# Interleaving the two chunks of a gating half, and weight buffers assigned by hand

## The chip, the core and the metric

The program runs on one core of a Trainium2 chip. The time is the device time of one execution in microseconds (us). The engines are named as in the profile: PE is the matrix engine (PEld its weight loads), DVE the vector engine, ACT the scalar engine, POOL is GpSimd, SP the engine that issues most transfers.

## What is computed

Two layers of a decoder trunk on 512 tokens of width 1024, all in float32. The change is in the second layer's token mixer, a chunked gating unit:

```python
def chunked_sgu_mixer(h, w_in, ln_g, ln_b, w_spatial, b_spatial, w_out):
    z = jax.nn.gelu(h @ w_in, approximate=False)      # 512 x 1024 @ 1024 x 4096
    u, v = jnp.split(z, 2, axis=-1)
    v = layer_norm(v, ln_g, ln_b)
    mixed = einsum('gts,bcsgd->bctgd', tril(w_spatial), vg) + b_spatial   # 128 x 128 per group
    return (u * mixed) @ w_out                         # 512 x 2048 @ 2048 x 1024
...
# every mixer is followed by:  x + square(relu(h @ w_up)) @ w_down
```

## The kernel before

A float32 product is made of three passes over pairs of fp32r tiles: a high part (`wh`, a cast on ACT, line 125) and a low part (`wl`, a subtraction on DVE, line 122). This is called a split. A large product is done by a seven-product scheme (as Strassen and Winograd), so the work is a list of items. One item multiplies a half-size block, 24 steps of 512 columns or 48 of 256, and needs one weight block of 1 MB (128x2048): loaded by SP, or loaded and then changed by a second transfer that adds another block into it (`add`, issued by POOL), and then split. Sums of products are carried in eight PSUM banks in pairs A, B, C, E. The split tiles `wh` and `wl` have three buffers each, so the split of item j can begin when item j-3 has left PE.

The gating layer (`sgu`, 502.95 us to about 798 us of the span) is 42 items: 0 to 13 the gate half `v` in two chunks of 1024 columns (`gate(0)`, `gate(1)`), 14 to 27 the other half (`other(0)`, `other(1)`), 28 to 41 the output product (`outer`). `prepare` of item j+2 follows `go` of item j in the program. Between items stand steps of the list `then`: `begin` (transposes and splits of the second half of the inputs, `gx1.rest`), the mixing matrix, the deviations, `normalised`, `mixed_tile`, `gated`, and at 40 `gx2.first`, which prepares the next layer's input. Before, the order is

```python
work = g0[:1] + g1[:1] + g0[1:] + g1[1:] + u0 + u1 + dn
```

Raw weight blocks live in a rotating list `raws`: two buffers shared by all layers (`raw_tile`, written R1 and R2 here), one of the layer's own (W), and from item 27 on two halves of `v[1]`. A `get` takes the head of the list, a `put` after the last split appends. `gate(1)` loads its first block, releases it after one item, and loads the same block again for item 9 (`p1` under `if c`).

The last layer (`ffn(1)`) takes its first block (name b) from R1, its second (a) from R2, and the third (c) from its own memory, which lies where the gating layer's tiles were. Item a is a load, an `add` and a split; after it come a sum a += b on DVE, an `add` into b, an `add` into a.

The instructions of each engine stand in one queue and leave it in order. What that order is, the framework's scheduler decides at build time by its own estimates; the program order is its priority. So a load may stand ahead of one that the program names earlier. An instruction waits at the head of its queue until its data and its buffer are ready.

Of the kernel before, what the change touches and what calls it, by code (L numbers as in the profile page):

```python
# [17 lines left out]
P = 128  # L18
# [39 lines left out]
def trunk(ctx: ExitStack, tc: tile.TileContext, a):  # L58
# [914 lines left out]
    class Slots:  # L973
# [5 lines left out]
        def get(self):  # L979
            return self.free.pop(0)  # L980

        def put(self, t):
            self.free.append(t)
# [7 lines left out]
    def ffn(layer, xq, norm, pool, after=None, last=None, mid=None):  # L991
# [7 lines left out]
        w_up, w_dn = a["ffn_w_up"][layer], a["ffn_w_down"][layer]  # L999
        r2, nr2 = small(), small()  # L1000
        raws = Slots(
            [raw_tile((P, 4, 512)) for _ in range(2)]
            + [pool.tile([P, 4, 512], F32, name=nm("wb")) for _ in range(4)]
        )
# [153 lines left out]
        def down(c, sq):  # L1158
# [9 lines left out]
            def fetch(name, k, u):  # L1168
                s[name] = raws.get()
                load(s[name], w(k, u))  # L1170
# [155 lines left out]
    with stage(1), tc.tile_pool(name="sgu", bufs=1) as sg:  # L1326
# [9 lines left out]

        names = ("a11", "a12", "a21", "a22")
        uq = [
            {t: sg.tile([P, 4, H], F32, name=nm("u")) for t in names},
            {t: v[0][:, n, :].rearrange("p (k n) -> p k n", k=4) for n, t in enumerate(names)},  # L1340
        ]
        raws = Slots(
            [raw_tile((P, 4, 512)) for _ in range(2)] + [sg.tile([P, 4, 512], F32, name=nm("wb"))]
        )
        banks = [psum() for _ in range(8)]
# [10 lines left out]

        def staged(i):
            return v[1][:, 2 * i : 2 * i + 2, 512:].rearrange("p a (b t) -> p a b t", t=P)

# [4 lines left out]
        def mix_load():  # L1364
            for gg in range(2):
                nc.gpsimd.dma_start(wsp[:, gg], ws_src[:, gg * 4 : gg * 4 + 4, :])
                nc.gpsimd.dma_start(
                    v[1][:, 2 + gg, 512:], bs_src[gg * 512 : (gg + 1) * 512].partition_broadcast(P)
                )
# [27 lines left out]

        def get(name, src):
            s[name] = raws.get()
            load(s[name], src)  # L1400

        def weights(w, name, make, free, shift=0):

            make()
            w.extend(split(wtiles(4, 512, shift), s[name]))
            if free:
                raws.put(s.pop(name))

        def rows_item(acc, first, left, name, make, free, end, late=None):

            w, l = [], []

            def prepare():
                l.extend(left())
                weights(w, name, make, free)
                if late is not None:
                    late()
# [12 lines left out]

        def cols_item(acc, first, right, name, make, free, end):

# [13 lines left out]

            return lambda: weights(w, name, make, free, 16), go

        norms = {}


        def gate(c, X, Y, Z):
            def w(k, u):
# [28 lines left out]
            def end2():  # L1482
                plus("a11", Z)
                gelu("a11", "r")
# [4 lines left out]
            def end3():  # L1489
                pass  # L1490

            def end6():
                keep("a12", X)
                plus("a12", Y)
                gelu("a12", "nr")
# [7 lines left out]

            def p1():
                if c:
                    get("a", w(0, 0))
                add(s["a"], w(0, 1))

            def p2():
                nc.vector.tensor_add(s["a"], s["a"], s["b"])  # L1510

            def item(acc, first, left, *args):
                return rows_item(acc, first, lambda: getattr(gx1, left), *args)

            return [
                item(X, True, "A11", "d" if c else "a",
                     lambda: get("d" if c else "a", w(0, 0)), bool(c), end1),
                item(Z, True, "A12", "c", lambda: get("c", w(1, 0)), True, end2),
                item(Y, True, "N1", "a", p1, False, end5),
                item(Y, False, "S4", "b", lambda: get("b", w(1, 1)), False, end3, p2),  # L1520
                item(X, False, "S2", "a", lambda: None, False, end6),
                item(X, False, "S3", "b", lambda: add(s["b"], w(0, 1)), True, end7),
                item(X, False, "A22", "a", lambda: add(s["a"], w(1, 0)), True, end4),
            ]


        def other(c, X, Y, Z):
            u = uq[c]

            def w(i, k):  # L1530
# [52 lines left out]
            def p1():  # L1583
                get("a", w(1, 0))
                add(s["a"], w(1, 1))

            def p2():
                nc.vector.tensor_add(s["a"], s["a"], s["b"])

            return [  # L1590
                cols_item(X, True, "A11", "b", lambda: get("b", w(0, 0)), False, end1),
                cols_item(Y, True, "S3", "a", p1, False, end5),
                cols_item(Z, True, "A12", "c", lambda: get("c", w(0, 1)), True, end2),
                cols_item(X, False, "S2", "a", p2, False, end6),
                cols_item(X, False, "N1", "b", lambda: add(s["b"], w(1, 0)), True, end7),
                cols_item(Y, False, "A22", "a", lambda: add(s["a"], w(0, 1)), True, end3),
                cols_item(X, False, "S4", "c", lambda: get("c", w(1, 1)), True, end4),
            ]
# [26 lines left out]
        def outer(X, Y, Z):  # L1625
# [31 lines left out]

            def product(acc, first, left, name, make, free, end, extra=None, late=None):
                for h in range(2):
                    def lefts(h=h):  # L1660
                        if extra is not None:
                            extra(h)
                        pairs.append(pairs.pop(0))
                        return split(pairs[-1], q[h][left])

                    items.append(rows_item(
                        acc, first and h == 0, lefts, f"{name}{h}", lambda h=h: make(h), free,
                        end if h else lambda: None,
                        (lambda h=h: late(h)) if late is not None else None,
                    ))  # L1670

            def put(n, k, u):
                return lambda h: get(f"{n}{h}", w(k, h, u))

# [3 lines left out]
            def p2(h):  # L1678
                nc.vector.tensor_add(s[f"a{h}"], s[f"a{h}"], s[f"b{h}"])

            product(X, True, "a11", "a", put("a", 0, 0), False, lambda: accumulate(X, 0, 0, 1))
            product(
                Z, True, "a12", "c", put("c", 1, 0), True, lambda: accumulate(Z, 0, 0, 1, True)
            )
            product(
                Y, True, "n1", "a", sum_("a", 0, 1), False, lambda: accumulate(Y, 1, 1, -1), n1
            )
            product(
                Y, False, "a12", "b", put("b", 1, 1), False, lambda: accumulate(Y, 0, 1, -1), s4, p2
            )  # L1690
            product(
                X, False, "a11", "a", lambda h: None, False, lambda: accumulate(X, 0, 1, -1, True)
            )
            product(
                X, False, "a21", "b", sum_("b", 0, 1), True, lambda: accumulate(X, 1, 1, -1, True)
            )
            product(
                X, False, "a22", "a", sum_("a", 1, 0), True, lambda: accumulate(X, 1, 0, 1, True)
            )
            return items  # L1700

        g0, g1 = gate(0, A, E, C), gate(1, B, E, C)
        u0, u1 = other(0, A, E, C), other(1, C, E, A)
        dn = outer(A, C, E)
        work = g0[:1] + g1[:1] + g0[1:] + g1[1:] + u0 + u1 + dn
        then = {}
# [41 lines left out]
        after(0, begin)  # L1748
        after(1, lambda: banks_are(C))
        after(4, rows_of_r)  # L1750
        after(5, lambda: (mix_transposed(0), mix_transposed(1)))
        after(6, lambda: (mix_shifts(0), mix_shifts(1)))
        after(7, lambda: banks_are(A))
        after(13, deviations)
        after(13, lambda: banks_are(B))
        after(14, lambda: normalised(0))
        for n in range(4):
            after(15 + n, lambda n=n: (mixed_tile(2 * n), mixed_tile(2 * n + 1)))
        after(18, lambda: normalised(1))
        after(18, lambda: gated(0, "a11"))  # L1760
        after(19, lambda: gated(0, "a22"))
        after(19, lambda: gated(0, "a21"))
        after(20, lambda: gated(0, "a12"))
        for n in range(4):
# [139 lines left out]
```

## Time and profile before

| what | value |
|---|---|
| median of 3 runs (lowest, highest) | 1138.94 us (1131.7, 1139.84) |
| the profiled execution: time, span | 1138.21 us, 1136.5 us |
| PE busy, DVE busy, ACT busy | 95%, 76%, 55% of the span |
| mean granted clock of PE | 0.973 |
| memory read | 161.27 MB |

1.7 us of the profiled time lie outside the span. A clock of 1.00 in the views is 2.4 GHz, 0.50 is 1.2 GHz.

### The profile page before, as it was taken

The page shows a single profiled execution, that of the slowest core. Times are in us where ns is not written, and L with a number is a line of the kernel's source. Part 1 is how long each engine was busy: PE and PEld are TensorE (multiplying, and loading weights), DVE is VectorE, ACT ScalarE, POOL GpSimd, SP SyncE. Part 2 cuts the span into 40 slices and gives each one's busy share as a digit, 9 for nine tenths or more (in the row PEclk, how much of TensorE's full clock was granted, in tenths as well). Part 3 has the DMA queues.
Part 4 walks back from the last instruction along what each step waited for, and adds up shares of the span by engine and source line. Part 5 has one row for each costly group of instructions (what it writes and reads, how often), then busy time and mean ns, then how long its engine had stood idle before and what let it go on. Part 6 is the DMA issues. An engine that isn't in the chain of part 4 may idle for free. (4 is left out here: it accounts for less than half of the span.)

```text
span 1136.5 us, 15747 instructions
## 1 busy us (share of the span) xinstructions
PE 1074.1 (95%) x6540; PEld 957.3 (84%) x6540; DVE 866.0 (76%) x947; ACT 628.8 (55%) x714; POOL 129.0 (11%) x155
## 2 busy tenths in 40 slices
PE   8799998999999999998798999899689999999997
PEld 6688888999999999876576999688689999999986
DVE  6988757887887878878656679796679788788753
ACT  4577636665555556466445645355656565555541
POOL 5510000000010010011001000010010101001000
PEclk9999999999999999998999899899889999999999
DMA  6121148659768777452946865467567876866431
GB/s 196 38 75 37 39 111 245 169 142 223 179 125 215 186 148 186 92 139 67 215 87 153 196 128 149 147 115 219 147 171 163 198 178 137 220 158 112 111 111 56
DMA packets 86611, 164.38 MB, mean 145 GB/s; under 512 B 4933, under 2 KB 10636, under 8 KB 86412
## 3 DMA queue, kind: packets, MB, share of 16 engines
q0 software_dynamic: 33584, 67.11, 33.7%
q1 hardware_dynamic: 52956, 96.27, 24.9%
q8 instruction: 51, 0.84, 0.3%
q14 instruction: 20, 0.16, 0.0%
HBM read 161.27 MB, written 2.10 MB: 144 GB/s over the span
## 5 line engine op out<-in xcount | busy, mean ns | idle before, releaser
L110 PE MATMUL ps<-g,wh 128*128 128x256 f32 (+1 forms) x2304 | 423.3, 286 | 10.4 <-DVE g L122 3.9
L110 PEld LDWEIGHTS ps<-g,wh 128*128 128x128 f32 x2304 | 362.3, 191 | 17.8 <-DVE g L122 4.4
L110 PE MATMUL ps<-g,wl 128*128 128x256 f32 (+1 forms) x1152 | 328.0, 285 | 3.5 <-DVE wl L122 3.5
L110 PE MATMUL ps<-wh,q 128*128 128x512 f32 (+1 forms) x840 | 266.5, 390 | 2.4 <-DVE x L1154 2.4
L122 DVE TENSOR_TENSOR wl<-wr,wh 128x2048 fp32r<-128x2048 f32 (+1 forms) x79 | 176.3, 2235 | 68.1 <-ACT wh L125 68.1
L110 PEld LDWEIGHTS ps<-g,wl 128*128 128x128 f32 x1152 | 218.8, 190 | 5.5 <-DVE wl L122 4.3
L122 DVE TENSOR_TENSOR wl<-wb,wh 128x2048 fp32r<-128x2048 f32 x74 | 169.5, 2290 | 62.8 <-ACT wh L125 62.7
L125 ACT CAST wh<-wr 128x2048 fp32r<-128x2048 f32 (+1 forms) x79 | 146.9, 1862 | 108.1 <-PE ps L110 40.7
L125 ACT CAST wh<-wb 128x2048 fp32r<-128x2048 f32 x74 | 141.1, 1907 | 109.6 <-PE ps L110 82.5
L110 PEld LDWEIGHTS ps<-wh,q 128*128 128x128 f32 x840 | 158.1, 189 | 34.3 <-issue 2.8
L110 PE MATMUL ps<-wh,g 128*128 128x512 f32 x496 | 164.5, 408 | 15.6 <-ACT wh L125 9.7
L110 PE MATMUL ps<-wl,q 128*128 128x512 f32 (+1 forms) x420 | 163.8, 390 | 0.0
L110 PEld LDWEIGHTS ps<-wh,g 128*128 128x128 f32 x496 | 97.0, 197 | 41.6 <-ACT wh L125 11.6
L125 ACT CAST q<-sq 128x1024 fp32r<-128x1024 f32 x51 | 53.5, 1050 | 90.5 <-PE ps L110 87.8
L110 PE MATMUL ps<-wl,g 128*128 128x512 f32 x248 | 101.0, 407 | 2.6 <-DVE wl L122 2.6
L110 PEld LDWEIGHTS ps<-wl,q 128*128 128x128 f32 x420 | 79.4, 189 | 14.7
L1154 DVE SCALAR_TENSOR_TENSOR x<-ps,s,x 128x512 f32<-128x512 f32 x98 | 72.7, 747 | 20.9 <-PE ps L110 20.9
L122 DVE TENSOR_TENSOR q<-sq,q 128x1024 fp32r<-128x1024 f32 x51 | 62.4, 1224 | 5.2 <-ACT q L125 2.3
L110 PEld LDWEIGHTS ps<-wl,g 128*128 128x128 f32 x248 | 48.7, 197 | 14.1 <-DVE wl L122 3.3
L989 POOL DMA_DIRECT2D wr<-in_ffn_w_up x16 | 20.9, 1308 | 265.8 <-DMA wr<-in_ffn_w_up 103.9
L989 POOL DMA_DIRECT2D wb<-in_ffn_w_down x17 | 21.9, 1291 | 131.3 <-DVE wl L122 129.5
L1071 DVE TENSOR_TENSOR sq<-sq,ps 128x512 f32<-128x512 f32 x48 | 32.6, 683 | 2.5 <-PE ps L110 1.3
(263 smaller groups left out, 1261.5 us busy)
## 6 DMA issues: line engine op xcount, KB each, us to landing
wb<-in_ffn_w_up SPq DMA_DIRECT2D x18, 1024.0 KB, 5.6
wb<-in_ffn_w_down SPq DMA_DIRECT2D x17, 1024.0 KB, 5.3
wb<-in_ffn_w_down POOLq DMA_DIRECT2D x17, 1024.0 KB, 9.2
wr<-in_ffn_w_up POOLq DMA_DIRECT2D x16, 1024.0 KB, 8.6
wr<-in_ffn_w_up SPq DMA_DIRECT2D x14, 1024.0 KB, 5.4
wr<-in_sgu_w_in SPq DMA_DIRECT2D x11, 1024.0 KB, 5.5
wr<-in_sgu_w_in POOLq DMA_DIRECT2D x10, 1024.0 KB, 9.6
wr<-in_ffn_w_down SPq DMA_DIRECT2D x9, 1024.0 KB, 6.2
```

The costliest lines, as they stand in the source:

```text
L110: nc.tensor.matmul(out, lhsT=lhsT, rhs=rhs, start=start and t == 0, stop=stop and t == 2, **kw)
L122: return eng.tensor_sub(l, src, h.bitcast(F32))
L125: nc.scalar.copy(hl[0], src)
L989: nc.gpsimd.dma_start(t, src, accum_op=ALU.add)
L1071: both(name, lambda t, j: nc.vector.tensor_add(t, t, pv(acc[sums][j])))
L1154: nc.vector.scalar_tensor_tensor(out=xs, in0=ps, scalar=r[:, i : i + 1], in1=xs, op0=ALU.mult, op1=ALU.add)
```

## The change

The gate half's items of the two chunks alternate (`gate(0)` item 1, `gate(1)` item 1, `gate(0)` item 2, ...). Each chunk keeps its two bank pairs to itself (A and E, B and C); the second and the third product share the second pair, so the copy for a12 is made one product earlier. `gate(1)` no longer loads its first block twice. The list `raws` of this layer is gone: each block has a buffer by name. W serves c of both chunks in turn; the second-step blocks b0, b1 lie in U1, U2, the two halves of the tile of `other(0)`'s results, in which `begin` has scratch before that; `outer` uses W, the tile `Bt` (BT) after its last use, R1, R2, and the halves of `v[1]`. So R1 and R2 have their last split at items 30 and 31. The mixing matrix is staged in another corner of `v`; the steps between items move by up to four places in the list. In the first feed-forward layer, the last `down` takes its blocks from the layer's own buffers where one is free (`get_but`).

```diff
@@ -979,6 +979,11 @@
         def get(self):
             return self.free.pop(0)
 
+        def get_but(self, others):
+
+            k = next((k for k, t in enumerate(self.free) if not any(t is o for o in others)), 0)
+            return self.free.pop(k)
+
...
@@ -998,9 +1003,9 @@
 
         w_up, w_dn = a["ffn_w_up"][layer], a["ffn_w_down"][layer]
         r2, nr2 = small(), small()
+        shared = [raw_tile((P, 4, 512)) for _ in range(2)]
         raws = Slots(
-            [raw_tile((P, 4, 512)) for _ in range(2)]
-            + [pool.tile([P, 4, 512], F32, name=nm("wb")) for _ in range(4)]
+            shared + [pool.tile([P, 4, 512], F32, name=nm("wb")) for _ in range(4)]
         )
...
@@ -1166,7 +1171,8 @@
             acc = {"X": banks[4:6], "Y": banks[6:8], "Z": banks[2:4] if alone else banks[6:8]}
 
             def fetch(name, k, u):
-                s[name] = raws.get()
+
+                s[name] = raws.get_but(shared if alone else ())
                 load(s[name], w(k, u))
 
             def w11():
...
+        u0 = sg.tile([P, NT, 1024], F32, name="u0")
         uq = [
-            {t: sg.tile([P, 4, H], F32, name=nm("u")) for t in names},
-            {t: v[0][:, n, :].rearrange("p (k n) -> p k n", k=4) for n, t in enumerate(names)},
+            {t: o[:, n, :].rearrange("p (k n) -> p k n", k=4) for n, t in enumerate(names)}
+            for o in (u0, v[0])
         ]
-        raws = Slots(
-            [raw_tile((P, 4, 512)) for _ in range(2)] + [sg.tile([P, 4, 512], F32, name=nm("wb"))]
-        )
+
+        def halves_of(t):
+            return [
+                t[:, 2 * n : 2 * n + 2, :].rearrange("p a (b c) -> p (a b) c", b=2)
+                for n in range(2)
+            ]
+
+
+        R1, R2 = (raw_tile((P, 4, 512)) for _ in range(2))
+        W = sg.tile([P, 4, 512], F32, name=nm("wb"))
+        U1, U2 = halves_of(u0)
+        V1, V2 = halves_of(v[1])
+        BT = Bt.rearrange("p (k a) t -> p k (a t)", k=4)
...
-        def staged(i):
-            return v[1][:, 2 * i : 2 * i + 2, 512:].rearrange("p a (b t) -> p a b t", t=P)
+        def staged(c):
+            return v[c][:, 2:4, 0:512].rearrange("p a (b t) -> p a b t", t=P)
...
-        def get(name, src):
-            s[name] = raws.get()
-            load(s[name], src)
-
-        def weights(w, name, make, free, shift=0):
+        def get(name, slot, src):
...
-        def gate(c, X, Y, Z):
+        def gate(c, X, Y, slots):
+            sa, sb, sc = slots
+            na, nb = f"a{c}", f"b{c}"
+
...
             def end2():
-                plus("a11", Z)
+                plus("a11", Y)
                 gelu("a11", "r")
...
             def end3():
-                pass
+                keep("a12", Y)
 
             def end6():
-                keep("a12", X)
-                plus("a12", Y)
+                plus("a12", X)
                 gelu("a12", "nr")
...
-            def p1():
-                if c:
-                    get("a", w(0, 0))
-                add(s["a"], w(0, 1))
-
             def p2():
-                nc.vector.tensor_add(s["a"], s["a"], s["b"])
+                nc.vector.tensor_add(s[na], s[na], s[nb])
...
-                item(X, True, "A11", "d" if c else "a",
-                     lambda: get("d" if c else "a", w(0, 0)), bool(c), end1),
-                item(Z, True, "A12", "c", lambda: get("c", w(1, 0)), True, end2),
-                item(Y, True, "N1", "a", p1, False, end5),
-                item(Y, False, "S4", "b", lambda: get("b", w(1, 1)), False, end3, p2),
-                item(X, False, "S2", "a", lambda: None, False, end6),
-                item(X, False, "S3", "b", lambda: add(s["b"], w(0, 1)), True, end7),
-                item(X, False, "A22", "a", lambda: add(s["a"], w(1, 0)), True, end4),
+                item(X, True, "A11", na, lambda: get(na, sa, w(0, 0)), end1),
+                item(Y, True, "A12", "c", lambda: get("c", sc, w(1, 0)), end2),
+                item(Y, True, "N1", na, lambda: add(sa, w(0, 1)), end5),
+                item(Y, False, "S4", nb, lambda: get(nb, sb, w(1, 1)), end3, p2),
+                item(X, False, "S2", na, lambda: None, end6),
+                item(X, False, "S3", nb, lambda: add(sb, w(0, 1)), end7),
+                item(X, False, "A22", na, lambda: add(sa, w(1, 0)), end4),
...
-        def other(c, X, Y, Z):
+        def other(c, X, Y, Z, slots):
             u = uq[c]
+            sa, sb, sc, sd = slots
...
+                cols_item(X, True, "A11", "b", lambda: get("b", sb, w(0, 0)), end1),
+                cols_item(Y, True, "S3", "a", p1, end5),
+                cols_item(Z, True, "A12", "c", lambda: get("c", sc, w(0, 1)), end2),
+                cols_item(X, False, "S2", "a", p2, end6),
+                cols_item(X, False, "N1", "b", lambda: add(sb, w(1, 0)), end7),
+                cols_item(Y, False, "A22", "a", lambda: add(sa, w(0, 1)), end3),
+                cols_item(X, False, "S4", "d", lambda: get("d", sd, w(1, 1)), end4),
...
-            def product(acc, first, left, name, make, free, end, extra=None, late=None):
+            slots = {"a0": W, "a1": BT, "c0": R1, "c1": R2, "b0": V1, "b1": V2}
+
+            def product(acc, first, left, name, make, end, extra=None, late=None):
...
-        g0, g1 = gate(0, A, E, C), gate(1, B, E, C)
-        u0, u1 = other(0, A, E, C), other(1, C, E, A)
-        dn = outer(A, C, E)
-        work = g0[:1] + g1[:1] + g0[1:] + g1[1:] + u0 + u1 + dn
+        work = [
+            i for two in zip(gate(0, A, E, (R1, U1, W)), gate(1, B, C, (R2, U2, W))) for i in two
+        ]
+        work += other(0, A, E, C, (R1, W, R2, W)) + other(1, C, E, A, (R2, R1, W, R1))
+        work += outer(A, C, E)
...
         after(0, begin)
-        after(1, lambda: banks_are(C))
-        after(4, rows_of_r)
-        after(5, lambda: (mix_transposed(0), mix_transposed(1)))
-        after(6, lambda: (mix_shifts(0), mix_shifts(1)))
-        after(7, lambda: banks_are(A))
+        after(6, lambda: banks_are(E))
+        after(8, rows_of_r)
+        after(9, lambda: (mix_transposed(0), mix_transposed(1)))
+        after(10, lambda: (mix_shifts(0), mix_shifts(1)))
         after(13, deviations)
         after(13, lambda: banks_are(B))
-        after(14, lambda: normalised(0))
+        after(15, lambda: normalised(0))
         for n in range(4):
-            after(15 + n, lambda n=n: (mixed_tile(2 * n), mixed_tile(2 * n + 1)))
-        after(18, lambda: normalised(1))
+            after(16 + n, lambda n=n: (mixed_tile(2 * n), mixed_tile(2 * n + 1)))
         after(18, lambda: gated(0, "a11"))
+        after(19, lambda: normalised(1))
         after(19, lambda: gated(0, "a22"))
-        after(19, lambda: gated(0, "a21"))
+        after(20, lambda: gated(0, "a21"))
         after(20, lambda: gated(0, "a12"))
         for n in range(4):
             after(21 + n, lambda n=n: (mixed_tile(8 + 2 * n), mixed_tile(9 + 2 * n)))
@@ -1767,10 +1769,6 @@
         after(25, lambda: gated(1, "a22"))
         after(26, lambda: gated(1, "a21"))
         after(27, lambda: gated(1, "a12"))
-        after(27, lambda: [
-            raws.put(v[1][:, 2 * n : 2 * n + 2, :].rearrange("p a (b c) -> p (a b) c", b=2))
-            for n in range(2)
-        ])
```

In `outer`, items keep their order; only where the blocks lie is changed.

## Rows read from the trace of the kernel before

**Rows 1.** Stretches of the span, busy time of each engine, granted clock (first line: columns).

```profile
core 0: us, PE busy (x) PEld busy (x) DVE busy (x) ACT busy (x) POOL busy (x), PEclk, DMA share, GB/s
502.95:528.00 25.05, 21.67 (x90) 17.23 (x91) 21.01 (x24) 17.67 (x25) 6.81 (x7) 0.86 0.50 166
528.00:616.00 88.00, 76.11 (x334) 60.25 (x333) 52.98 (x61) 41.05 (x42) 7.76 (x6) 0.94 0.60 132
616.00:632.00 16.00, 12.54 (x86) 12.34 (x85) 7.38 (x7) 10.20 (x10) 3.69 (x3) 0.79 0.84 175
632.00:723.00 91.00, 91.00 (x734) 88.09 (x732) 80.04 (x71) 43.62 (x37) 6.44 (x5) 1.00 0.68 177
706.70:717.60 10.90, 10.90 (x50) 9.05 (x50) 10.90 (x11) 4.88 (x4) 0.83 (x1) 1.00 1.10 241
723.00:735.00 12.00, 7.28 (x20) 5.12 (x19) 5.94 (x4) 6.46 (x4) 0.00 (x0) 0.72 0.03 12
798.00:842.00 44.00, 29.79 (x224) 28.57 (x224) 28.98 (x28) 26.48 (x30) 2.58 (x2) 0.84 0.54 131
842.00:1130.00 288.00, 287.59 (x1821) 260.76 (x1819) 217.47 (x178) 156.42 (x141) 24.91 (x21) 1.00 0.62 150
170.00:203.00 33.00, 29.14 (x211) 27.62 (x210) 25.97 (x32) 21.19 (x31) 2.58 (x2) 0.95 0.80 223
```

**Rows 2.** Same view, PE alone: two of six half-clock stretches, and the sum of six.

```profile
569.00:573.90 4.90, 4.86 (x12) 0.50 0.05 19
...
823.30:829.90 6.60, 4.60 (x18) 0.50 0.10 7
sum 28.80, PE 26.62; mean PE 4.44
```

**Rows 3.** Same view, PE alone: half-clock stretches at two stage starts.

```profile
520.50:526.10 5.60, 5.59 (x13) 0.50 0.01 3
195.30:198.40 3.10, 3.05 (x14) 0.50 1.07 187
```

**Rows 4.** PE's waits, 528 to 632 us: total, times, longest.

```profile
PE ps L110 <- ACT wh L125: 4.9, 1, 4.9
PE ps L110 <- DVE wl L122: 4.2, 3, 1.6
PE ps L1605 <- ACT v L1740: 3.5, 1, 3.5
```

**Rows 5.** Timeline of SP, GpSimd, ScalarE: start, us, what [idle before, releaser].

```profile
550.34 0.37 SPq L986 DMA_DIRECT2D wr<-in_sgu_w_in  x1
556.19 1.28 POOL L989 DMA_DIRECT2D wr<-in_sgu_w_in  x1 [13.41 <-DMA wr<-in_sgu_w_in]
567.09 1.90 ACT L125 CAST wh<-wr 128x2048 fp32r<-128x2048 f32 x1 [5.43 <-DMA wr<-in_sgu_w_in]
```

**Rows 6.** Timelines: two loads of one buffer, its cast, a split on VectorE.

```profile
502.95 0.37 SPq L986 DMA_DIRECT2D wb<-in_sgu_w_in  x1
510.18 1.91 ACT L125 CAST wh<-wb 128x2048 fp32r<-128x2048 f32 x1 [2.70 <-DMA wb<-in_sgu_w_in]
514.45 0.37 SPq L986 DMA_DIRECT2D wb<-in_sgu_w_in  x1
528.57 2.29 DVE L122 TENSOR_TENSOR wl<-wr,wh 128x2048 fp32r<-128x2048 f32 x1
```

**Rows 7.** Timeline of ScalarE in the last part of the gating layer.

```profile
725.14 1.90 ACT L125 CAST wh<-v 128x2048 fp32r<-128x2048 f32 x1 [6.45 <-DMA v<-in_sgu_w_out]
```

**Rows 8.** Timelines at the start of the last layer, four engines.

```profile
780.15 0.37 SPq L986 DMA_DIRECT2D wr<-in_ffn_w_up  x1
786.23 1.30 POOL L989 DMA_DIRECT2D wr<-in_ffn_w_up  x1 [22.35 <-DMA wr<-in_ffn_w_up]
800.59 1.90 ACT L125 CAST wh<-wr 128x2048 fp32r<-128x2048 f32 x1 [10.04 <-DMA wr<-in_ffn_w_up]
805.86 0.68 DVE L1640 TENSOR_TENSOR x<-x,ps 128x512 f32<-128x512 f32 x1
```

More of the change, by code (lines that the diff above doesn't have):

```diff
@@ L1367, in mix_load @@
                 nc.gpsimd.dma_start(
-                    v[1][:, 2 + gg, 512:], bs_src[gg * 512 : (gg + 1) * 512].partition_broadcast(P)
+                    v[1][:, 2 + gg, 0:512], bs_src[gg * 512 : (gg + 1) * 512].partition_broadcast(P)
                 )
@@ L1396, in trunk, with weights, rows_item @@
         s = {}
-        def get(name, src):
-            s[name] = raws.get()
-            load(s[name], src)
-        def weights(w, name, make, free, shift=0):
+        def get(name, slot, src):
+            s[name] = slot
+            load(slot, src)
+        def weights(w, name, make, shift=0):
             make()
             w.extend(split(wtiles(4, 512, shift), s[name]))
-            if free:
-                raws.put(s.pop(name))
-        def rows_item(acc, first, left, name, make, free, end, late=None):
+        def rows_item(acc, first, left, name, make, end, late=None):
             w, l = [], []
@@ L1414, in prepare @@
                 l.extend(left())
-                weights(w, name, make, free)
+                weights(w, name, make)
                 if late is not None:
@@ L1429, in rows_item, with cols_item @@
             return prepare, go
-        def cols_item(acc, first, right, name, make, free, end):
+        def cols_item(acc, first, right, name, make, end):
             w = []
@@ L1445, in go @@
                 end()
-            return lambda: weights(w, name, make, free, 16), go
+            return lambda: weights(w, name, make, 16), go
         norms = {}
-        def gate(c, X, Y, Z):
+        def gate(c, X, Y, slots):
+            sa, sb, sc = slots
+            na, nb = f"a{c}", f"b{c}"
             def w(k, u):
@@ L1583, in p1 @@
             def p1():
-                get("a", w(1, 0))
-                add(s["a"], w(1, 1))
+                get("a", sa, w(1, 0))
+                add(sa, w(1, 1))
             def p2():
-                nc.vector.tensor_add(s["a"], s["a"], s["b"])
+                nc.vector.tensor_add(sa, sa, sb)
             return [
[L1591 to L1597, printed above, removed]
+                cols_item(X, True, "A11", "b", lambda: get("b", sb, w(0, 0)), end1),
[5 more added lines that the diff above has]
+                cols_item(X, False, "S4", "d", lambda: get("d", sd, w(1, 1)), end4),
             ]
@@ L1666, in product @@
                     items.append(rows_item(
-                        acc, first and h == 0, lefts, f"{name}{h}", lambda h=h: make(h), free,
+                        acc, first and h == 0, lefts, f"{name}{h}", lambda h=h: make(h),
                         end if h else lambda: None,
@@ L1672, in put @@
             def put(n, k, u):
-                return lambda h: get(f"{n}{h}", w(k, h, u))
+                return lambda h: get(f"{n}{h}", slots[f"{n}{h}"], w(k, h, u))
             def sum_(n, k, u):
@@ L1679, in p2 @@
                 nc.vector.tensor_add(s[f"a{h}"], s[f"a{h}"], s[f"b{h}"])
[L1681 to L1699, printed above, removed]
-            return items
-        g0, g1 = gate(0, A, E, C), gate(1, B, E, C)
-        u0, u1 = other(0, A, E, C), other(1, C, E, A)
-        dn = outer(A, C, E)
-        work = g0[:1] + g1[:1] + g0[1:] + g1[1:] + u0 + u1 + dn
+            product(X, True, "a11", "a", put("a", 0, 0), lambda: accumulate(X, 0, 0, 1))
+            product(Z, True, "a12", "c", put("c", 1, 0), lambda: accumulate(Z, 0, 0, 1, True))
+            product(Y, True, "n1", "a", sum_("a", 0, 1), lambda: accumulate(Y, 1, 1, -1), n1)
+            product(Y, False, "a12", "b", put("b", 1, 1), lambda: accumulate(Y, 0, 1, -1), s4, p2)
+            product(X, False, "a11", "a", lambda h: None, lambda: accumulate(X, 0, 1, -1, True))
+            product(X, False, "a21", "b", sum_("b", 0, 1), lambda: accumulate(X, 1, 1, -1, True))
+            product(X, False, "a22", "a", sum_("a", 1, 0), lambda: accumulate(X, 1, 0, 1, True))
+            return items
+        work = [
[3 more added lines that the diff above has]
+        work += outer(A, C, E)
         then = {}
```

## Prediction, made before the changed kernel ran

> **What bounds the kernel now.** I read the table first: PE is busy for 95% of the span, so the question is where the other 5% lie and how far this change reaches them. The timeline of PE, cut into stretches, answers that [rows 1]: the reader is to take busy time from length. From 842 to 1130 us PE idles for 0.4 us in 288, and from 632 to 723 us not at all; there no other engine matters, although DVE is busy for 80.04 of 91. The idle time sits in and beside the gating layer: 3.38 us at its start (502.95 to 528), 11.89 in the rest of the gate half (to 616), 3.46 at the first mixed tiles (to 632), 4.72 in the output product (723 to 735), 14.21 at the start of the last layer (798 to 842). The second thing to see is the granted clock in the same lines, below 1.00 in just these stretches: after an idle stretch PE works at 1.2 GHz for some microseconds. Fitted closely to the half-clock time there are six such stretches behind the start; PE works for 26.62 us in them and so does 13.31 us less work than at 2.4 GHz [rows 2]. At the layer's start it is 5.59 / 2 = 2.80 us [rows 3].
>
> Then the waits say what ended the idle time [rows 4], and the timelines of the queues say why that came late.
>
> **The change part by part.** An item takes 10.90 / 2 = 5.45 us of PE (two items from 706.7 to 717.6 [rows 1]). A split is a cast of 1.90 and a subtraction of 2.29 us, 4.2 in all [rows 5, 6]; it can begin three items ahead of its own, so two items, 10.9 us, hide it. A load took 502.95 to 510.18, 7.2 us [rows 6]; an add 556.19 to 567.09, 10.9 us [rows 5].
>
> Gate half, behind its start. The longest wait, 4.9 us, is for the cast of a block [rows 4]: gate(1)'s first block again, loaded at 550.34 when its buffer came free, added to at 556.19, cast at 567.09 after 5.43 us of idle ACT [rows 5]. The change keeps the block, so the load is gone and the add can start in the first items. The three waits for a low part (4.2 us) are sums and adds that one chunk's next item needs at once; with the other chunk's item between, each chain has twice the time, 10.9 us more, which is a whole add. The copies out of banks (the rest of the 11.89) have an item between them too. One 1 MB load less; copies and additions are as many as before, a12's only one product earlier. I take all 11.89.
>
> The start itself. PE waits there for the splits of the inputs, which stay. New is that item 3 is gate(1)'s A12, whose block c uses W after gate(0)'s. In the trace W is loaded again at 514.45, just when it is free [rows 6]; with c0's 7.2 us it lands at 521.7, and with 4.2 for the split it is ready at 525.9. Item 2 ends at about 528. So nothing, if DVE takes the split at once. But DVE has 21.01 us of work in that stretch of 25.05 [rows 1], and the first free split stands at 528.57 [rows 6]; there it would end at 530.9, 2.9 late, and an idle stretch could bring the half clock with it as at 195.3, 3.05 / 2 = 1.5 [rows 3]. Ends: 4.4 lost, and 6.2 gained if the blocks' new order lets the inputs' splits through and the start's 3.38 + 2.80 vanish. I take 1.6 lost, nearest to DVE's row. Behind SP's c1 stand b0 and b1, whose buffers U1, U2 are scratch until those splits; they are needed at items 6 and 7, three items later, so their wait costs nothing unless they stand ahead of c1.
>
> First mixed tiles. PE waits 3.5 us for `normalised` [rows 4]. `mixed_tile` moves behind one more item, 5.45 us: covered. I take 3.46. But the buffers by name make loads tight here: item 15's block a uses R1 after item 12's split, which can begin when item 9 ends; split, load, add, split are 4.2 + 7.2 + 10.9 + 4.2 = 26.5 us, and items 10 to 14 are 27.3. Ends: nothing, and one late block as at 567.09, 4.9 idle and 4.86 / 2 of clock, 7.3 in all [rows 2, 4]. I take 2.0: the chain fits, barely, and the transfers share the memory with others. The other reloads of that half have about one item more.
>
> Output product. The cast at 725.14 waits 6.45 us for a block in a half of `v` [rows 7], a buffer that came free late. That block, c1, goes to R2, whose former block has its split for item 26, five items ahead: 27 us against 7.2 + 4.2. a1 in BT can load after the last mixed tile behind item 24, also five items ahead. b0, b1 in the halves of `v` are for items 34 and 35. I take 4.72.
>
> Last layer. Block a loads at 780.15, when R2 is free; the add goes out at 786.23 and lands 14 us later, with other loads beside it; ACT waits 10.04 us for it, DVE behind ACT, and behind a's split on DVE stands the last addition to x, 805.86, for which PE's transposes wait [rows 8]. The sum a += b and the adds after it come late in turn. R2 free at item 31 instead of 41 is 54 us earlier, so block a should stand ready. POOL's queue puts its add behind those of the output product; that still leaves it ahead of its use. What remains is then what the first layer shows at the same place, with its blocks in good time: 33.00 - 29.14 = 3.86 idle and 1.53 of clock, 5.39 [rows 1, 3].
>
> `get_but`: two blocks of the first feed-forward layer move to other buffers, in items that PE covers; nothing.
>
> **The sum.** Idle 11.89 + 3.46 + 4.72 + 14.21 = 34.28; clock 13.31; less 5.39 that stay: 42.2 gained. Lost 1.6 and 2.0. Net 38.6: from the profiled 1138.21 to 1099.6, I say 1100. The median of the runs is 0.7 above the profiled one, which I leave out. What follows, 842 to 1130, has PE idle for 0.4 us, so the gain reaches the end.
>
> The Trainium skill (TensorE: Matmul & The Clock Gate, Terms) prices a lowered clock as half of all the time spent at it. By the clocks of the stretches that is 5.3 + 3.4 + 3.4 + 7.0 = 19.0 us [rows 1] instead of 13.31, and the sum would be 1094; the trace shows idle time inside these stretches, which is counted already, so the rows' value stands.
>
> **Rivals.** (1) The start of the last layer stays as it is: c, its third block, lies under Bt and cannot load before the last split of a1 there, and SP's queue holds what stands behind. Against it: SP sits at R2's load until 780.15 now as well, and c is needed two items after a. The 12.5 us gained there (14.21, some 3.7 of the clock's 13.31, less 5.39) fall away: 1112. (2) The gate half fills with other waits: ACT or DVE hold a ready split behind one whose block has not landed. ACT's 10.04 us [rows 8] speak for it; against it, 632 to 723, where DVE is as full and PE never idle. Half of the gate's 11.89 and 2.43 of clock (the stretch at 569 [rows 2]) and the start's 4.4 instead of 1.6: 1110. The Trainium skill (the same page, on the engines' queues) calls ACT's and DVE's queues strictly first in, first out; by that rule this rival's time holds as soon as one cast stands too early. (3) The start's stall goes too, and the tight loads cost nothing: 1099.6 - 7.8 - 2.0, 1090. (4) The change doesn't do what it says: the scheduler's new order of the queues gives back what is gained: 1138. (5) Slower: buffers by name. Before, a `get` takes whichever block is free; after it, seven blocks of items 15 to 27 each wait for one named buffer. From the point where the chain of 26.5 us passes 27.3, each costs 7.3 us, together 51 - 2: 1149.
>
> **How the numbers follow.** A measurement here tells about 1% (11.4 us) from no change. Forecast 1094 to 1106: 0.47. Rival 1: 0.14, rival 2: 0.14, rival 3: 0.08, rival 4: 0.10, rival 5: 0.07. Faster by over 1% (below 1127.5) are the forecast and rivals 1 to 3: 0.83; same 0.10; slower 0.07. Range: 1090 to 1120 takes in all four of these and both ends of the unknown costs; it leaves out rivals 4 and 5, 0.17.
>
> **What would show it.** Right: one load of 1 MB less from the gate's weights; no wait of PE for a cast in the gate half; the mixed tiles without a wait; ACT without a long wait for a transfer at the start of the last layer, and PE's transposes there without one; the clock at 1.00 from the gate's second pair of items to the last layer. Wrong: a wait of PE for c1's split at item 3 over 4 us; waits for casts in items 15 to 21; the add of the last layer's block a on POOL behind something late.

## The result, and the profile after

The changed kernel takes 1097.05 us, median of 4 runs (1092.3 to 1099.8), against 1138.49 of the kernel before: ratio 0.9643, 95% interval 0.9592 to 0.9694, some 41 us. A second measurement, beside the experiments below, gave 0.9641 (0.962 to 0.9662). The forecast was 1100, range 1090 to 1120. Memory read falls from 161.27 to 160.22 MB: the block of 1 MB that is no longer loaded twice.

The profiled execution took 1099.80 us (span 1098.1), 38.4 less than the one of before. The same view as [rows 1], with the same columns, cut where the stages of the changed kernel begin and end:

```profile
502.95:531.00 28.05, 22.62 (x99) 17.52 (x98) 22.18 (x25) 21.05 (x28) 5.91 (x7) 0.94 0.72 198
531.00:592.00 61.00, 61.00 (x262) 49.28 (x261) 48.53 (x56) 34.22 (x37) 6.49 (x5) 0.97 0.67 150
592.00:620.00 28.00, 28.00 (x232) 27.61 (x231) 18.95 (x18) 20.93 (x20) 4.93 (x4) 1.00 0.81 177
620.00:707.00 87.00, 85.19 (x652) 82.27 (x651) 72.11 (x64) 40.33 (x33) 5.16 (x4) 0.98 0.62 171
707.00:720.00 13.00, 13.00 (x59) 10.78 (x58) 12.91 (x11) 7.11 (x5) 1.30 (x1) 1.00 0.69 167
768.00:800.00 32.00, 29.28 (x244) 28.05 (x242) 30.26 (x32) 25.72 (x31) 2.58 (x2) 1.00 0.74 190
800.00:1092.00 292.00, 291.14 (x1850) 264.17 (x1848) 218.38 (x179) 157.25 (x143) 24.91 (x21) 1.00 0.62 148
```

Read as before, length less PE: the start of the gating layer now idles 5.43 us (3.38 before), the rest of the gate half none in 61 us (11.89), the first mixed tiles none, the other half 1.81, the output product none (4.72), the start of the last layer 2.72 (14.21). In all 9.96 us where it was 37.66: 27.7 of the 38.4. The clock is 1.00 in the last layer's start, which was at 0.84. In these parts PE still works at half clock in two stretches, both behind an idle one:

```profile
528.20:533.70 5.50, 5.48 (x13) 0.50 0.79 260
626.50:629.90 3.40, 3.40 (x19) 0.50 0.44 119
```

That is about 2.7 and 1.7 us of work lost, where the seven stretches of before lost 13.31 + 2.80 = 16.1 [rows 2, 3]: another 11.7. Idle time and clock together give 39.4; about 1 us net is lost elsewhere. Ahead of the gating layer, for one, this execution has more work at half clock than the one of before (12.07 us of PE from 193.0 to 199.9 and 486.5 to 493.5, against 6.55 from 195.0 to 198.4 and 488.5 to 492.0). A second execution of the same kernel (as_changed below) does not, so that is not the change's doing.

The waits of PE that are left, besides 2.0 us at the start for the splits of the inputs (timeline of PE; the last is a row of the last layer's start, where two of 0.78 and 0.89 us follow):

```profile
528.22 0.80 PE L110 MATMUL ps<-wl,g 128*128 128x512 f32 x1 [3.44 <-DVE wl L122]
625.20 0.50 PE L110 MATMUL ps<-g,wh 128*128 128x256 f32 x2 [1.81 <-ACT u L1550]
770.92 0.50 PE L110 MATMUL ps<-g,wh 128*128 128x256 f32 x2 [1.02 <-ACT g L125]
```

The first is gate(1)'s block c at item 3. Its way through the queues, SP, ACT and DVE, with c of gate(0) first in the same buffer:

```profile
503.34 0.37 SPq L991 DMA_DIRECT2D wb<-in_sgu_w_in  x1
512.06 1.91 ACT L125 CAST wh<-wb 128x2048 fp32r<-128x2048 f32 x1 [4.21 <-DMA wb<-in_sgu_w_in]
516.32 0.37 SPq L991 DMA_DIRECT2D wb<-in_sgu_w_in  x1
521.85 1.91 ACT L125 CAST wh<-wb 128x2048 fp32r<-128x2048 f32 x1 [0.63 <-DMA wb<-in_sgu_w_in]
525.88 2.29 DVE L122 TENSOR_TENSOR wl<-wb,wh 128x2048 fp32r<-128x2048 f32 x1
```

W is loaded twice in turn, as forecast. The first load took 503.34 to 512.06, 8.7 us where it took 7.2 [rows 6]. Adds of POOL went out ahead of it at 494.07 and 500.55, where before there was one, at 495.01; that the second add made the load longer is not shown. So the second load could start only at 516.32, was cast at 521.85, and its low part, behind the splits of the inputs on DVE, began at 525.88; PE waited for it until 528.22.

The wait at 625.20 is for a copy out of a bank on ACT. Timeline of SP and ACT:

```profile
612.41 0.37 SPq L991 DMA_DIRECT2D wb<-in_sgu_w_in  x1
622.77 1.90 ACT L125 CAST wh<-wb 128x2048 fp32r<-128x2048 f32 x1 [2.58 <-DMA wb<-in_sgu_w_in]
624.57 0.58 ACT L1550 COPY u<-ps 128x512 f32<-128x512 f32 x1
```

The cast of the other half's block d stood ahead of the copy and waited 2.58 us for a transfer that had been 10 us under way. At the start of the last layer, block a and its add (SP, then POOL):

```profile
701.24 0.37 SPq L991 DMA_DIRECT2D wr<-in_ffn_w_up  x1
712.81 1.30 POOL L994 DMA_DIRECT2D wr<-in_ffn_w_up  x1 [21.19 <-DMA wr<-in_ffn_w_up]
723.45 1.29 POOL L994 DMA_DIRECT2D v<-in_sgu_w_out  x1 [9.34 <-DVE x L1652]
```

They are there 79 and 73 us earlier than in [rows 8]; about 30 us of that is the layer's own earlier start (768 us, before 798). POOL's queue has the add ahead of the output product's adds from 723.45 on, not behind them.

### The profile page after: what moved, and what is told of

Read it like the earlier page. It is cut to its first block, busy times and chain, and to the rows that moved or that the text cites. A ratio compares the mean times of both kernels' runs of the same rounds, so it can differ in the third digit from the quotient of the medians.

```text
span 1098.1 us, 15748 instructions
## 1 busy us (share of the span) xinstructions
PE 1062.3 (97%) x6540; PEld 950.8 (87%) x6540; DVE 865.7 (79%) x947; ACT 628.7 (57%) x714; POOL 128.3 (12%) x155
## 3 DMA queue, kind: packets, MB, share of 16 engines
HBM read 160.22 MB, written 2.10 MB: 148 GB/s over the span
## 4 chain that ended last, share of the span: by engine, by line
PE 84%; DVE 7%; DMA 3%; ACT 3%; issue 2%; POOL 0%; SPq 0%; POOLq 0%; ACTq 0%; DVEq 0%
PE ps L110 79%; DVE wl L122 2%; DMA wb<-in_sgu_w_in 2%; ACT wh L125 2%; PE ps L1617 1%; DVE g L122 1%; PE ps L856 1%; DMA wb<-in_ffn_w_up 1%; DVE sq L485 1%; PE ps L296 1%; ACT p L836 0%; ACT v L1743 0%; PE ps L826 0%; PE ps L824 0%; PE ps L823 0%
## 5 line engine op out<-in xcount | busy, mean ns | idle before, releaser
L122 DVE TENSOR_TENSOR wl<-wb,wh 128x2048 fp32r<-128x2048 f32 x75 | 171.7, 2289 | 69.8 <-ACT wh L125 69.8
L122 DVE TENSOR_TENSOR wl<-wr,wh 128x2048 fp32r<-128x2048 f32 (+1 forms) x69 | 153.3, 2225 | 38.0 <-ACT wh L125 38.0
L125 ACT CAST wh<-wr 128x2048 fp32r<-128x2048 f32 (+1 forms) x69 | 127.8, 1855 | 69.9 <-PE ps L110 49.9
L110 PE MATMUL ps<-wh,g 128*128 128x512 f32 x496 | 158.2, 397 | 2.1 <-DVE g L122 1.3
L110 PEld LDWEIGHTS ps<-wh,g 128*128 128x128 f32 x496 | 94.2, 190 | 23.6 <-DVE g L122 1.7
L110 PE MATMUL ps<-wl,g 128*128 128x512 f32 x248 | 98.1, 396 | 3.4 <-DVE wl L122 3.4
```

The costliest lines, as they stand in the source:

```text
L110: nc.tensor.matmul(out, lhsT=lhsT, rhs=rhs, start=start and t == 0, stop=stop and t == 2, **kw)
L122: return eng.tensor_sub(l, src, h.bitcast(F32))
L125: nc.scalar.copy(hl[0], src)
```

## The experiments

Each kernel ran beside the kernel before on the same chip; "more" and "less" compare ratios, each of which carries some 0.002 to 0.004 either way, so differences under about 4 us are not settled by time alone. 0.0010 is 1.1 us. For the changed kernel I take the second measurement, 0.9641.

**order_before**: the gate half in the order of before, all else as changed.

```diff
-        work = [
-            i for two in zip(gate(0, A, E, (R1, U1, W)), gate(1, B, C, (R2, U2, W))) for i in two
-        ]
+        g0, g1 = gate(0, A, E, (R1, U1, W)), gate(1, B, C, (R2, U2, W))
+        work = g0[:1] + g1[:1] + g0[1:] + g1[1:]
...
+        after(1, lambda: banks_are(C))
+        after(4, rows_of_r)
+        after(5, lambda: (mix_transposed(0), mix_transposed(1)))
+        after(6, lambda: (mix_shifts(0), mix_shifts(1)))
```

> The gate half's items in the order of before, the buffers by name and the rest as changed (so gate(1)'s first block is still kept). Theory A, each part has its own share: the waits that only the order removes come back, 11.89 less 4.9 idle = 7.0, and some 1.5 of clock, while the wait for gate(1)'s block c at the start goes (3.4 idle and some 3 of clock), so 1097 + 8.5 less about 5: 1098 to 1106. Rival B, the order is what removes all of the gate half's waits: 16 us come back, 1108 to 1114. Rival C, the order moves nothing: 1095 to 1099, and no waits of PE for a low part or a bank copy in the gate half.

Measured: 1108.49 us, ratio 0.9752 (0.9727 to 0.9777), 12.6 us more than changed. Theory A's sum was too small; rival B's number holds. PE alone, by stretches, the last two at half clock:

```profile
502.95:531.00 28.05, 25.36 (x108) 0.94 0.69 201
531.00:615.00 84.00, 72.90 (x343) 0.94 0.55 116
537.60:541.00 3.40, 3.40 (x9) 0.50 0.37 51
588.80:595.60 6.80, 4.24 (x10) 0.50 0.49 156
```

In the gate half behind its start PE so loses 11.10 us idle and 3.8 by the clock, 14.9, although the block is kept. The kernel before loses 15.8 there: 11.89 idle and 3.95 by the clock (3.04 us of PE at half clock from 550.0 to 553.4, 4.86 from 569.0 to 573.9). The start idles 2.69 us, where the changed kernel idles 5.43: c1's wait is gone with the order of before. The 12.6 us is what remains of the order's gain behind the start after its cost there.

The waits of PE in the gate half behind its start (total, times, longest), and the queues ahead of the longest of them, 5.2 us, which ended at 591.36 (POOL, ACT, DVE, DVE):

```profile
PE ps L110 <- DVE v L1487: 7.3, 2, 5.2
PE ps L110 <- ACT wh L125: 3.8, 3, 1.5
```

```profile
574.59 1.29 POOL L994 DMA_DIRECT2D wr<-in_sgu_w_in  x1 [2.38 <-DVE wl L122]
586.39 1.90 ACT L125 CAST wh<-wr 128x2048 fp32r<-128x2048 f32 x1 [4.06 <-DMA wr<-in_sgu_w_in]
588.32 2.29 DVE L122 TENSOR_TENSOR wl<-wr,wh 128x2048 fp32r<-128x2048 f32 x1 [4.63 <-ACT wh L125]
590.53 0.68 DVE L1487 TENSOR_TENSOR v<-v,ps 128x512 f32<-128x512 f32 x1
```

The add into a block goes out at 574.59 and lands 12 us later. ACT's cast waits for it, DVE's split (588.32) for the cast, and behind that split stands the addition that empties the bank PE needs next (590.53). A late block so stops PE through a bank and not through its own item. With the items alternating neither the block nor the bank is urgent.

**order_banks_before**: the same, with the banks of before too.

```diff
-                plus("a11", Y)
+                plus("a11", Z)
...
             def end3():
-                keep("a12", Y)
+                pass
...
             def end6():
-                plus("a12", X)
+                keep("a12", X)
+                plus("a12", Y)
...
-                item(Y, True, "A12", "c", lambda: get("c", sc, w(1, 0)), end2),
+                item(Z, True, "A12", "c", lambda: get("c", sc, w(1, 0)), end2),
...
+        g0, g1 = gate(0, A, E, C, (R1, U1, W)), gate(1, B, E, C, (R2, U2, W))
+        work = g0[:1] + g1[:1] + g0[1:] + g1[1:]
```

> As order_before, and also the gate half's banks as before: the second product in a third pair, a12 copied out on ACT one product later. Theory D, formed on order_before: there an addition out of a bank stood on DVE behind a split whose block was late, and PE waited for it (5.2 us at 591, 2.1 at 551); with the copy on ACT these two go, 4 to 8 us less than order_before. Rival: the late blocks alone set the waits, which then appear as waits for a cast or a low part, the same as order_before within 2 us.

Measured: 1105.75 us, ratio 0.9741 (0.9719 to 0.9763), 1.2 us less than order_before by ratio, with nearly 4 either way, so the time alone separates the two expectations poorly. The two long waits for an addition behind a split are gone, and PE's waits in the gate half fall from 11.1 to 7.0 us, at the lower end of theory D; but other waits came in their place, and the start idles 4.89 us again instead of 2.69, which takes up half of that:

```profile
PE ps L110 <- ACT v L1482: 3.3, 2, 2.5
PE ps L110 <- DVE wl L122: 1.6, 2, 1.3
PE ps L110 <- ACT wh L125: 1.3, 2, 0.7
PE ps L110 <- DVE v L1487: 0.8, 2, 0.5
```

With the new banks the order is worth 12.6 us (order_before against the changed kernel), with a12 copied out late as before some 8.7 (this run against no_swap, the next one): 9 to 13 us whichever way the banks are emptied. What the late blocks hold up changes, that they hold something up does not.

**no_swap**: the changed kernel, with a12 copied out one product later (the edits of `end3` and `end6` above).

> The changed kernel with a12 copied out one product later, as before; the items still alternate. Theory: with the other chunk's item between, either bank is free in time: the same as the changed kernel within 2 us. Rival: the earlier copy is what frees the bank, 3 us or more slower.

Measured: 1098.18 us, ratio 0.9664 (0.9643 to 0.9685), 2.6 us more; between the two expectations and inside the uncertainty. In its gate half PE has no wait behind item 3, as in the changed kernel; it has 2.81 us where the changed kernel has 1.81, at item 18. A gain from the earlier copy itself is not shown.

**order_before_reload**: order_before, and gate(1) loads its first block again.

```diff
-                item(Y, True, "N1", na, lambda: add(sa, w(0, 1)), end5),
+                item(Y, True, "N1", na, again if c else lambda: add(sa, w(0, 1)), end5),
...
-                item(X, False, "A22", na, lambda: add(sa, w(1, 0)), end4),
+                item(X, False, "A22", na, lambda: add(s[na], w(1, 0)), end4),
...
+            def again():
+                get(na, U1, w(0, 0))
+                add(U1, w(0, 1))
```

> As order_before, and gate(1) loads its first block a second time for its N1 item, into the buffer that gate(0)'s b leaves (U1), as late as in the kernel before. Theory A: PE's one wait for a cast comes back, 4.9 idle and 2.4 of clock, 7.3 more than order_before. Rival: other work covers the load, the same time as order_before within 2 us.

Measured: 1112.05 us, ratio 0.9788 (0.9765 to 0.9811), 4.1 us more than order_before by ratio: between the two. PE's waits in the same part:

```profile
PE ps L110 <- DVE v L1487: 11.3, 5, 4.6
PE ps L110 <- ACT wh L125: 2.4, 2, 1.3
```

No long wait for the block's own cast came back, but the waits for additions out of banks grew from 7.3 to 11.3 us: again the block's lateness reaches PE through DVE's queue (the longest, 4.6, stands behind the split of the reloaded block, for which ACT's cast at 566.29 waited 5.99 us). That the reload costs something in this order is likely; its size, 4.1 with some 2.5 either way, is under the 7.3 expected. It is not the reload of the kernel before: it goes into U1, and as a whole PE here idles 13.4 us in the gate half behind its start, more than before (11.89). What the reload would cost with the items alternating was not run.

**a1_in_r2**: R2 is held to the end of the gating layer.

```diff
-            slots = {"a0": W, "a1": BT, "c0": R1, "c1": R2, "b0": V1, "b1": V2}
+            slots = {"a0": W, "a1": R2, "c0": R1, "c1": BT, "b0": V1, "b1": V2}
```

> The output product's block a1 lies in R2 and c1 in Bt, so R2 has its last split at item 41 and not at 31; all else as changed. Theory A, the early release of R2 makes the start of the last layer: 7 to 12.5 us come back, 1104 to 1110, with ACT idle for block a's add and PE's transposes waiting for x. Rival: the last layer's start would be as good with a late block, since the first wait there was set by the queues' order: 1095 to 1099.

Measured: 1109.33 us, ratio 0.9767 (0.9742 to 0.9791), 14.3 us more. The chain of [rows 8] is back, link by link: block a's load on SP, ACT's cast, PE's transposes:

```profile
754.04 0.37 SPq L991 DMA_DIRECT2D wr<-in_ffn_w_up  x1
774.44 1.90 ACT L125 CAST wh<-wr 128x2048 fp32r<-128x2048 f32 x1 [9.98 <-DMA wr<-in_ffn_w_up]
780.45 0.90 PE L296 MATMUL ps<-ident,x 128*128 128x128 f32 x3 [7.04 <-DVE x L1652]
```

R2's early release makes the difference of the last layer's start: c1 in Bt, changed with it, costs nothing (PE is busy from 707 to 745 us).

**c1_in_v**: the output product's c1 in a half of `v`, as before.

```diff
-            slots = {"a0": W, "a1": BT, "c0": R1, "c1": R2, "b0": V1, "b1": V2}
+            slots = {"a0": W, "a1": BT, "c0": R1, "c1": V1, "b0": R1, "b1": V2}
```

> The output product's c1 lies in a half of v, free only after the gated step, as in the kernel before; b0 takes R1 after c0. Theory A: PE waits at item 31 for c1's cast, 4.7 idle and 2.7 of clock, 1102 to 1106. Rival: c1 was late because of the other transfers under way at that time and not because of its buffer; these are changed too, so 1095 to 1100.

Measured: 1103.47 us, ratio 0.9714 (0.9688 to 0.974), 8.3 us more. ACT waits for the block as in [rows 7], and PE for ACT:

```profile
702.98 1.90 ACT L125 CAST wh<-v 128x2048 fp32r<-128x2048 f32 x1 [6.44 <-DMA v<-in_sgu_w_out]
704.93 0.80 PE L110 MATMUL ps<-wh,g 128*128 128x512 f32 x1 [3.82 <-ACT wh L125]
```

So c1 is late through its buffer. b0's place was changed with it and was not tried alone.

**no_get_but**: the other edit of the shared buffers undone.

```diff
-                s[name] = raws.get_but(shared if alone else ())
+                s[name] = raws.get()
```

> The first feed-forward layer's last product takes its blocks from the head of the list again; all else as changed. Theory A: these items are covered, 1095 to 1099. Rival: the earlier release of R2 there is worth the wait at the gating layer's start, 2 to 5 us more.

Measured: 1093.94 us, ratio 0.9634 (0.9605 to 0.9664): no difference, theory A.

**mix_early**: the first chunk's normalising and mixed tiles an item earlier, as before.

```diff
-        after(15, lambda: normalised(0))
+        after(14, lambda: normalised(0))
         for n in range(4):
-            after(16 + n, lambda n=n: (mixed_tile(2 * n), mixed_tile(2 * n + 1)))
+            after(15 + n, lambda n=n: (mixed_tile(2 * n), mixed_tile(2 * n + 1)))
```

> normalised(0) and the mixed tiles of the first chunk one item earlier, as in the kernel before; all else as changed. Theory A, moving them behind one more item covers PE's wait of 3.5 us: with the step back, the wait comes back in part, 2 to 3.5 idle and up to 2.9 of clock, 1099 to 1104. Rival: the wait came from ACT and DVE being held by late blocks, which are gone, so the step's place costs nothing: 1095 to 1099.

Measured: 1091.62 us, ratio 0.9612 (0.9579 to 0.9646), 3.3 us less than changed, inside the uncertainty; in no case more. Theory A falls. PE does not wait at all around the mixed tiles, and the wait of item 18 is gone too (all engines, columns as in [rows 1]):

```profile
592.00:612.00 20.00, 20.00 (x171) 19.87 (x170) 13.22 (x15) 17.07 (x16) 4.93 (x4) 1.00 0.82 173
612.00:640.00 28.00, 28.00 (x242) 28.00 (x242) 23.71 (x23) 13.08 (x11) 0.00 (x0) 1.00 0.47 141
```

So, with the items alternating, the later place of the step is not what keeps the wait of [rows 4] for `normalised` away. What stood ahead of it in the kernel before, on ACT, DVE and PE:

```profile
610.91 1.91 ACT L125 CAST wh<-wr 128x2048 fp32r<-128x2048 f32 x1 [4.99 <-DMA wr<-in_sgu_w_in]
612.72 0.68 ACT L1474 ACTIVATE v<-ps,s 128x512 f32<-128x512 f32 x1
615.05 0.69 DVE L1477 BATCH_NORM_STATS2 stats<-v 128x6 f32<-128x512 f32 x1
625.98 1.22 PE L1605 MATMUL ps<-wt,v 128*128 128x128 f32 x4 [3.46 <-ACT v L1740]
```

The last part of `v` (612.72) and its statistics (615.05), which `normalised` needs, stood behind a cast that waited 4.99 us for its block. In mix_early no cast waits for a transfer in that part, which fits the rival; the late block was not put back there by itself.

**gate_c1_in_bt**: gate(1)'s c in a buffer of its own.

```diff
-            i for two in zip(gate(0, A, E, (R1, U1, W)), gate(1, B, C, (R2, U2, W))) for i in two
+            i for two in zip(gate(0, A, E, (R1, U1, W)), gate(1, B, C, (R2, U2, BT))) for i in two
```

> gate(1)'s block c lies in Bt, which is free until the mixing step, and not in W behind gate(0)'s c; all else as changed. Theory A: the wait at item 3 (3.44 us for c1's low part, and half the clock for some 6 us behind it) is that of W used twice; it goes, 3 to 6 us faster, 1091 to 1094. Rival: VectorE's queue is full there with the splits of the inputs, so the wait stays where it is or moves to the next item: 1095 to 1099.

Measured: 1090.97 us, ratio 0.9615 (0.9577 to 0.9653), 3.0 us less than changed. The wait for c1 (3.44) is gone; the splits of the inputs hold PE a little longer ahead of it (timeline of PE, items 2 and 3):

```profile
516.45 0.50 PE L110 MATMUL ps<-wh,g 128*128 128x512 f32 x1 [2.43 <-ACT g L125]
520.11 0.73 PE L110 MATMUL ps<-wh,g 128*128 128x512 f32 x1 [0.48 <-DVE g L122]
530.32 0.50 PE L110 MATMUL ps<-wl,g 128*128 128x512 f32 x1 [0.16 <-DVE wl L122]
```

Idle time there falls from 5.4 to 3.1 us. The time points the same way and its interval does not settle it.

**both_moved**: and block d of the other half in R2.

```diff
-        work += other(0, A, E, C, (R1, W, R2, W)) + other(1, C, E, A, (R2, R1, W, R1))
+        work += other(0, A, E, C, (R1, W, R2, R2)) + other(1, C, E, A, (W, R1, R2, R1))
-            slots = {"a0": W, "a1": BT, "c0": R1, "c1": R2, "b0": V1, "b1": V2}
+            slots = {"a0": BT, "a1": W, "c0": R1, "c1": R2, "b0": V1, "b1": V2}
```

> As gate_c1_in_bt, and the other half's block d, which PE waited for at 625 us (1.81 us and a half-clock stretch of 3.4), lies in R2 and not in W; u1's a and c and the output product's a0 and a1 change places to make room. Theory A: another 1.8 and 1.7 us, 1088 to 1091. Rival: the block was late because three transfers were under way at once, and they are still: the same as gate_c1_in_bt within 1.5 us.

Measured: 1093.43 us, ratio 0.9625 (0.9596 to 0.9654). PE's wait at item 18 is gone from its trace, yet the time is not below gate_c1_in_bt. There was little left to gain: in gate_c1_in_bt that wait is 1.0 us, with the clock at 1.00 behind it. Within the intervals neither expectation is settled.

**as_changed** and **c1_bt_mix_early**: the changed kernel again, and the two mends together (the edits of gate_c1_in_bt and mix_early).

> The changed kernel again, beside the others of this group, so that differences of a few us can be read: 0.962 to 0.966 of the kernel before.

> Two pieces of the changed kernel mended at once: gate(1)'s c in Bt, and normalised(0) and the first mixed tiles an item earlier. Theory: each takes out a wait of PE with its half-clock stretch of its own (3.4 us at item 3, 1.8 at item 18), so their gains add: 6 to 9 us less than the changed kernel. Rival: both end at the same bound, DVE's queue in that stretch, so together no more than the better one alone, 3 to 4 us.

Measured: 1095.36 us, ratio 0.9641 (0.962 to 0.9662), as expected, and 1090.90 us, ratio 0.9611 (0.9588 to 0.9634). The mends together give 3.4 us, about as much as either alone: the rival's number, though 3 us either way does not quite rule out the theory's 6. DVE's queue as their common bound is not what the trace shows; PE idles nowhere from item 4 to 700 us:

```profile
501.00:535.00 34.00, 30.97 (x135) 0.95 0.72 215
535.00:592.00 57.00, 57.00 (x268) 1.00 0.63 130
592.00:700.00 108.00, 108.00 (x850) 1.00 0.74 194
```

3.0 of the first 34 us are idle, at the splits of the inputs. The version is the fastest of the runs by median; that it beats the changed kernel is likely and, with intervals that overlap, not shown.

## Why the prediction was right

The sum was 42.2 us gained and 3.6 lost, net 38.6; the profiled executions differ by 38.4 and the medians by 41. By its steps:

- Gate half behind its start, all 11.89 idle and the clock with it: right, none is left. The shares were wrong: I had put nearly half of it on the reload. order_before keeps the block and still loses 14.9 of the 15.8 us there, so the order takes out nearly all of it: in the order of before other late blocks stop PE, also through banks that wait in DVE's queue. What the kept block is worth with the items alternating is not shown.
- The start, 1.6 lost: it is 2.0 (5.43 + 2.7 against 3.38 + 2.80). The mechanism is the one given, W used twice and DVE full; gate_c1_in_bt, with a second buffer, takes the wait at item 3 out.
- First mixed tiles, 3.46 gained: right in size, wrong in its reason. I named the later place of the step as the cover; mix_early shows that the place is worth nothing once the items alternate.
- Tight loads, 2.0 lost: 1.81 idle and 1.7 of clock, but for block d at item 18 through a bank copy, not for item 15's block a, for which PE does not wait.
- Output product: right, and c1_in_v returns 8.3 us for the 7.4 of idle and clock.
- Last layer, 12.5 gained: 15.2 (14.21 and 3.7 of clock, less 2.72). The term was too small by 2.7: the first layer, taken as what remains, idles 1.1 us more and has a half-clock stretch, 1.5, that the last layer now lacks. a1_in_r2 returns 14.3. That POOL's add would stand behind those of the output product was wrong, and is not seen to matter.
- `get_but`, nothing: right.

That the sum meets the profiled 38.4 to 0.2 us is luck in part: the last layer gave 2.7 more than its term, the tight loads cost 1.5 and the start 0.4 more, and the executions differ by about 1 us elsewhere. The changed kernel's four runs spread over 7.5 us.

Three parts undone one at a time, 12.6 (order), 8.3 (c1) and 14.3 (R2), make 35.2 of some 41 us. The reload's 4.1 belongs to the order of before and cannot be added to them.

Of the rivals, (1) and (2) did not come: c is loaded in time although it lies under Bt, and the gate half has no wait; a ready addition held behind a split whose block is late, which (2) is about, is what order_before shows. Nor did (4) come, with some 41 us gained. (5), slower, had no trace of its late blocks but one. Of (3), the start's stall stayed. Of the signs, the clock's failed: it fell behind the waits at items 3 and 18; c1's wait at item 3, 3.44 us, stayed under the 4 that would have counted against the forecast.

The Trainium skill's price for a lowered clock (TensorE: Matmul & The Clock Gate, Terms), half of all the time spent at it, would have made the sum 1094; the rows' price, PE's work in it alone, 1100. Between them lies the measured 1097; the runs spread too far to tell.

## What to carry to other kernels

When PE idles for a late block, look for a second independent chain of the same kind and alternate the two: it doubles the time that each load, add and split has, with no work more. A buffer that a later stage shares is best given to the items that finish early; here one 1 MB buffer free ten items sooner was worth 14 us. And when a wait goes away with a step that was moved, move the step back before crediting the move.

## What had not been expected of the hardware

A wait on one engine's queue shows up under another name: with the order of before, 7.3 us of PE's waits were for additions out of banks, and the longest of them, 5.2, traced back to a transfer that landed 12 us after it was issued.

The length of a short idle stretch does not tell what the clock does behind it. The wait for the copy out of a bank at item 18 is in several runs. In the changed kernel's trace it was 1.81 us, and the granted clock was 0.50 from 626.50 to 629.90. In as_changed it was 1.72 us, and in no_swap 2.81, and the clock stayed at 1.00 behind both. no_swap, PE's wait and the stretch behind it:

```profile
623.62 0.50 PE L110 MATMUL ps<-g,wh 128*128 128x256 f32 x2 [2.81 <-ACT u L1551]
623.60:640.00 16.40, 16.38 (x144) 1.00 0.55 161
```
